# Projection products of a hybrid S5 and DeltaNet layer, split by rows into two halves of TensorE's array

## The chip, the cores and the metric

The kernel runs on one core of one Trainium2 chip. The metric is the device time of one execution in microseconds. Three executions of the kernel before took 3030.34, 3026.27 and 3029.54 us: a median of 3029.54 us. A core has five engines that work at the same time, each with its own queue of instructions that it takes in order: PE (TensorE, matrix products; its loads of the stationary operand have a row of their own in the profile, PEld), DVE (VectorE), ACT (ScalarE), POOL (GpSimd) and SP (SyncE, which here issues the transfers). PE writes its products to PSUM, eight banks of 128 partitions by 512 float32 values; DVE and ACT read them from there.

## The reference

The layer maps x, 1024 frames of 2048 channels in float32, to an output of the same shape:

```python
h = rmsnorm(x, ln_w)
proj = h @ w_in                      # 2048 -> 2048 + 4096 + 16 + 4096 columns
(u_s, z_s, q, k, v, z_d, beta_l, a_l, gate_s, gate_d) = split(proj)
y_s = s5_mixer(u_s, z_s, ...) @ s5_w_up        # diagonal state space, GELU, y * sigmoid(y @ w_glu), * silu(z)
y_d = deltanet_mixer(q, k, v, z_d, ...) @ dn_w_up   # causal conv, delta rule in chunks, 8 heads x 128
mixed = sigmoid(gate_s) * y_s + sigmoid(gate_d) * y_d
out = rmsnorm(x + mixed @ w_out, final_norm_w)
```

So there are the large matrix products (`w_in`, `w_glu`, `s5_w_up`, `dn_w_up`, `w_out`), and between them two mixers made of many small products, scans and elementwise work.

## The kernel before

**Tiles.** The 1024 frames are done in two passes of 512 (`NPASS`, `T`). In a pass the projections are 128 output channels at a time: the stationary operand is a 128x128 block of a weight (128 input rows, 128 output columns), the moving operand 128 rows of the activations by 512 frames, and one PSUM bank (`pb`) gathers the sum over 16 row blocks (8 for the second-level products `ud`, `us`, `glu`). To keep nearly float32 accuracy with the one-pass type float32r, the weight and the activation are each split into a high and a low part, `wh + wl` and `mh + ml`, and each block takes three products, `wh*mh`, `wh*ml`, `wl*mh` (lines 1515 to 1517), each with a weight load of its own. Below, a *large product* is one of these: 128x128 stationary, 512 columns moving. Without the first tile `k` and the narrow tile `ba`, the projections of both passes have 159 tiles of 48 and 80 tiles of 24 large products: 9,552. The last stage, `mixed @ w_out` (lines 1606 to 1649), has 1,536 more, with the activations stationary.

**Weights.** `w_load` (line 393) brings half a tile's weight block of 512 KB by a DMA on SP's queue, with three buffers. `w_prep` (line 404) makes the high part on ACT (`whi`) and the low part on DVE (`wlo`), in chunks of four row blocks, at most four chunks ahead of PE (`LA`).

**Epilogues.** When a tile's sum is complete, ACT and DVE take it from its bank. `conv_epi` (q, k, v): ACT copies it to `xpad` and, scaled, to `acc`, then DVE adds three shifted terms. `silu_epi` (z): ACT makes a tanh from the bank, DVE multiplies with the bank. `s5_epi` (u): ACT copies with a reordering. `gd`, `gs`, `glu`: a tanh on ACT. `ud`, `us`: one DVE instruction. Tiles take banks 0 and 1 in turn (`mainb`), so one bank is emptied while PE fills the other.

**Mixers between the products.** The small work stands in generators: `s5_gen` (banks 6 and 7), `d_prep` (banks 5 and 2) and `d_chain` (banks 3 and 4). After each row block of a projection `pump` lets each lane do a step when the planner's own clocks (`Clock`, `Timed`) say that its inputs are there; `drain` forces the rest at fixed places. The order in every engine's queue is fixed when the program is built. Thus short products of the mixers stand between the large ones on PE, in its one queue. `d_prep` transposes k (`pK`), sums squares of q with a one-column product (`pQ`), and forms k*k and k*q (`pA`) and a blockwise inverse with products of 32 and 64 rows (`pG`, `pU`); `d_chain` carries the state through four chunks (`pA`, `pB`, `pC`). The S5 branch has two groups for each half of a block: `pV`, products of 64 rows that alternate between rows 0-63 and 64-127 of the array and between banks 6 and 7, and `pY`, a full-row product and products with 64 output columns.

The parts of the planner's cost table and of the steps that matter here:

```python
elif k["rhs"].dtype == F32R:
    c = n / 2400                     # us that the planner books for a large product
...
pb = bank(mainb[0] % 2)              # a tile's sum
...
pA = bank((5, 2)[hf])                # d_prep; pK, pV, pU in bank 2, pD, pQ, pG in bank 5
return bank((3, 4)[bi[0] % 2])       # d_chain: every product in the other bank
```

Of the kernel before, what the change touches and what calls it, by code (L numbers as in the profile page):

```python
# [93 lines left out]
class Timed:  # L94
# [3 lines left out]
    def __getattr__(self, name):  # L98
        f = getattr(self.eng, name)
        if name not in COST:  # L100
            return f

        def g(*a, **k):
            o = a[0]
            ck = self.clock
            n = o.free_size()
            ins = [v for v in a[1:] if isinstance(v, bass.AP)]
            ins += [v for kk, v in k.items() if isinstance(v, bass.AP) and kk != "accum_out"]
            outs = [o]
            if self.key == "PE":  # L110
                if name == "transpose":
                    c = 0.11
                elif k["rhs"].dtype == F32R:
                    c = n / 2400
                else:
                    rows = k["lhsT"].shape[0]
                    c = max(n / 600, 0.06) * (0.3 if o.shape[0] <= 32 else 0.5 if min(o.shape[0], rows) <= 64 else 1.0)
                lat = 0.1
            elif name == "dma_start":
                c, lat = 4.0 * n * o.shape[0], 0  # L120
            else:
# [12 lines left out]
            ck.run(self.key, c, outs, ins, lat, name == "dma_start")  # L134
            return f(*a, **k)  # L135
        return g
# [11 lines left out]
def kernel(  # L148
# [724 lines left out]
    def s5_epi(pb, t):  # L873

        u = s5w["u"].rearrange("p (e n) -> p e n", e=2)
        S.activation(u, pb.rearrange("p (n e) -> p e n", e=2), AF.Copy)
        yield
        for q in range(4):
            SP.dma_start(part(us_d, t * 65536 + q % 2 * 32768 + q // 2 * 256, (512, 32), (16384, 2), (1, 256)),
                         u[32 * q:32 * q + 32])  # L880
        done.add(("u", t))
        yield -1
# [207 lines left out]
    def d_prep(h, ps_):  # L1090
# [16 lines left out]
        yield from until((ps_, "q", h))  # L1107
        pK = bank(2)
        S.activation(LU, kq[:, :, 1, :], AF.Square)
# [18 lines left out]
        for hf in range(2):  # L1128
            pA = bank((5, 2)[hf])
            for c in (2 * hf, 2 * hf + 1):  # L1130
                PE.matmul(pA[:, (c % 2) * 256:(c % 2) * 256 + 256], lhsT=kq[:, c, 0, :],
                          rhs=kq[:, c].rearrange("p a n -> p (a n)"), start=True, stop=True)
            pa = pA.rearrange("p (c a n) -> p c a n", c=2, a=2)
            tt(LU[:, 2 * hf:2 * hf + 2, :], pa[:, :, 0, :], E[:, 2 * hf:2 * hf + 2, :], MUL)
            tt(qk[:, 2 * hf:2 * hf + 2, :], pa[:, :, 1, :], E[:, 2 * hf:2 * hf + 2, :], MUL)
            yield
# [30 lines left out]
        yield from until((ps_, "v", h))  # L1167
        pV = bank(2)
        for c in range(4):
# [17 lines left out]
        yield  # L1187
        pU = bank(2)
        for b in B4:
# [18 lines left out]
        yield  # L1208
        pU = bank(2)
        pu = pU.rearrange("p (c n) -> p c n", c=4)  # L1210
# [18 lines left out]
        yield  # L1229
        pU = bank(2)  # L1230
        pu = pU.rearrange("p (c n) -> p c n", c=4)
# [8 lines left out]
    def d_chain(h, ps_):  # L1240
# [18 lines left out]
        zz = kq[:, 0:2].rearrange("p c a n -> p (c a n)")  # L1259
        bi = [0]  # L1260

        def bk():
            bi[0] += 1
            return bank((3, 4)[bi[0] % 2])
        for c in range(4):
# [109 lines left out]
    for ps_ in range(NPASS):  # L1375
# [39 lines left out]
        def silu_epi(pb, dst, split):  # L1415
            S.activation(th, pb, AF.Tanh, scale=0.5)
            yield
            if split:
                stt(eo(tx), by_step(th), 1.0, by_step(pb), ADD, MUL)
            else:  # L1420
                stt(tx, th, 1.0, pb, ADD, MUL)
            later(dst, tx)
            yield -1

        for kind, i, c0 in plan[ps_]:
# [22 lines left out]
            if not (ps_ == 0 and kind == "k" and i == 0):  # L1448
                pb = bank(mainb[0] % 2)
                mainb[0] += 1  # L1450
            if ps_ == 0 and kind == "ba":
                pk0 = bank(1)
                mainb[0] += 1

# [3 lines left out]
                for z in range(2):  # L1458
                    PE.matmul(pb[0:32, :], lhsT=ztile[:, 0:32], rhs=ztile, start=(z == 0), stop=False)
                    PE.matmul(pk0, lhsT=ztile[:, 0:P], rhs=ztile, start=(z == 0), stop=False)  # L1460
# [12 lines left out]
                for n, (kt, t0, nt) in enumerate(steps):  # L1473
# [17 lines left out]
                    wh, wl = hi[:, kl * P:(kl + 1) * P], lo[:, kl * P:(kl + 1) * P]  # L1491
                    PE.matmul(pb[0:32, cs], lhsT=h3[:, kl, 0:32], rhs=mh, start=False, stop=False)
                    PE.matmul(pb[0:32, cs], lhsT=h3[:, kl, 0:32], rhs=ml, start=False, stop=(n + 1 == len(steps)))
                    PE.matmul(pk0[:, cs], lhsT=wh, rhs=mh, start=False, stop=False)
# [3 lines left out]
            elif ps_ == 0 and kind == "k" and i == 0:  # L1498
                nkt, pb = 0, pk0
            for k4 in range(nkt // 4):  # L1500
                hi, lo = w_next()
                if kind == "ba":
                    h3 = hi.rearrange("p (k c) -> p k c", k=4)
                    for kl in range(4):
                        kt = k4 * 4 + kl
                        mh, ml = mov(kind, kt)
                        PE.matmul(pb[0:32, :], lhsT=h3[:, kl, 0:32], rhs=mh, start=(kt == 0), stop=False)
                        PE.matmul(pb[0:32, :], lhsT=h3[:, kl, 0:32], rhs=ml, start=False, stop=(kt == nkt - 1))
# [26 lines left out]
            if kind == "ba":  # L1535
                lgr = dw["set"][1]["kd"].rearrange("p c n -> p (c n)")[0:32, :] if ps_ == 0 else \
                    s5w["AB"][0:32, 0:512]
                S.activation(lgr, pb[0:32, :], AF.Copy)
                add("prep", -1, gates_prep(lgr, ps_))
# [28 lines left out]
            elif kind == "gd":  # L1568
                S.activation(q4[i % 2], pb, AF.Tanh, scale=0.5)
                later(td_d[i], q4[i % 2])  # L1570
            elif kind == "gs":
                S.activation(eo(q4[i % 2]), by_step(pb), AF.Tanh, scale=0.5)
                later(ts_d[i], q4[i % 2])
            elif kind == "ud":
                stt(mixed[:, i, :], q4[i % 4], 1.0, pb, ADD, MUL)
            elif kind == "glu":
                S.activation(q4[0], pb, AF.Tanh, scale=0.25)
                yh, yl = kt_of(yg, i)
# [5 lines left out]
            elif kind == "us":  # L1584
                stt(q4[3], q4[i % 3], 1.0, pb, ADD, MUL)
                tt(by_step(mixed[:, i, :]), by_step(mixed[:, i, :]), eo(q4[3]), ADD)
# [96 lines left out]
```

## Time and profile before

| What | Value |
|---|---|
| Median of three executions | 3029.54 us |
| Profiled execution, its own time | 3029.73 us |
| Its span, first to last instruction | 3027.8 us |
| Mean granted TensorE clock | 0.993 |
| PE busy | 2974.2 us, 98% |
| PEld busy | 2391.6 us, 79% |
| DVE busy | 1662.4 us, 55% |
| ACT busy | 1152.2 us, 38% |
| POOL busy | 449.3 us, 15% |
| PE's share of the chain that ended last | 85% |

The span is 1.9 us shorter than the execution's own time. A PE instruction's time in the profile runs from its start to its modelled end, and PE starts the next one before that end; what an instruction costs in a row of equal ones is thus the distance between two starts, which the timeline of the trace gives, not its mean duration. The timeline merges equal instructions that follow each other into one row with their count. The name of a row is what is written, an arrow, and what is read: `p<-X,whi` is a product into a PSUM bank from the activations in X and a high weight. `128*128 128x512` is rows by columns of the array that it uses, then the moving operand's rows by columns; all compute instructions carry the line of one recording helper, L135. A float32 product (not float32r) of the mixers stands in the trace as two PE instructions.

### The profile page before, as it was taken

What the parts mean: (1) busy time and instruction counts of PE and PEld (TensorE: products, weight loads), DVE (VectorE), ACT (ScalarE), POOL (GpSimd) and SP (SyncE); (2) the same over time, 40 slices, a digit from 0 to 9 for tenths busy, and PEclk for the clock granted to TensorE, in tenths of its full rate; (3) what the DMA queues carried; (4) which work ended last, traced back from release to release, by engine and by line L of the source; (5) the groups of instructions that cost most, each with busy time, mean ns of one, the idle gap of its engine ahead of it and who ended that gap; (6) DMA issues with size and microseconds to landing.
All of it is one profiled execution on the core that took longest, in us unless ns stands there. A gap on an engine that the chain in (4) does not pass through costs nothing.

```text
span 3027.8 us, 42544 instructions
## 1 busy us (share of the span) xinstructions
PE 2974.2 (98%) x16030; PEld 2391.6 (79%) x16030; DVE 1662.4 (55%) x3082; ACT 1152.2 (38%) x2483; POOL 449.3 (15%) x857
## 2 busy tenths in 40 slices
PE   8989999999999999999999999999999999999998
PEld 6877777777777888888878777777777788888887
DVE  5746676777777522553454575567557633226542
ACT  5434544554454222334333333333433322223331
POOL 4412222122200000000033221222112000000000
PEclk9999999999999999999999999999999999999999
DMA  6525444444445644446354344444444464445541
GB/s 168 133 57 154 122 121 130 111 117 122 133 135 166 191 122 120 144 134 238 119 160 134 108 114 115 133 114 117 119 126 120 123 207 122 122 122 153 197 151 56
DMA packets 582143, 405.02 MB, mean 134 GB/s; under 512 B 55161, under 2 KB 515122, under 8 KB 580018
## 3 DMA queue, kind: packets, MB, share of 16 engines
q1 hardware_dynamic: 579634, 393.92, 45.3%
q0 software_dynamic: 2304, 8.39, 0.8%
q8 instruction: 126, 2.06, 0.3%
q14 instruction: 79, 0.65, 0.1%
HBM read 335.66 MB, written 66.58 MB: 133 GB/s over the span
## 4 chain that ended last, share of the span: by engine, by line
PE 85%; DVE 7%; POOL 2%; ACT 2%; issue 1%; DMA 1%; SPq 0%; DVEq 0%; POOLq 0%; ACTq 0%
PE p L135 85%; DVE G0a L135 2%; POOL M L135 2%; DVE M L135 2%; DVE wlo L135 1%; DVE tmp L135 1%; ACT M L135 1%; DMA raw<-in_w_in_dram 0%; DVE Y L135 0%; POOL smalls L135 0%; DMA M<-tu_d 0%; SPq L135 0%; ACT whi L135 0%; ACT L135 0%; ACT tmp L135 0%
## 5 line engine op out<-in xcount | busy, mean ns | idle before, releaser
L135 PE MATMUL p<-X,whi 128*128 128x512 f32 (+1 forms) x4432 | 1398.7, 398 | 1.9 <-DVE whi L135 0.8
L135 DVE TENSOR_TENSOR wlo<-raw,whi 128x512 fp32r<-128x512 f32 x920 | 631.0, 698 | 700.9 <-ACT whi L135 700.1
L135 PEld LDWEIGHTS p<-X,whi 128*128 128x128 f32 (+1 forms) x4432 | 802.8, 188 | 177.1 <-issue 19.9
L135 PE MATMUL p<-X,wlo 128*128 128x512 f32 (+1 forms) x2184 | 854.2, 391 | 8.0 <-DVE wlo L135 7.9
L135 ACT ACTIVATE whi<-raw 128x512 fp32r<-128x512 f32 x917 | 557.7, 625 | 512.6 <-PE p L135 485.0
L135 PE MATMUL p<-Y,whi 128*128 128x512 f32 (+1 forms) x1808 | 568.8, 396 | 1.9 <-ACT whi L135 1.1
L135 PEld LDWEIGHTS p<-X,wlo 128*128 128x128 f32 x2184 | 411.7, 189 | 97.6 <-DVE wlo L135 9.1
L135 PEld LDWEIGHTS p<-Y,whi 128*128 128x128 f32 (+1 forms) x1808 | 329.9, 187 | 72.8 <-ACT whi L135 2.6
L135 PE MATMUL p<-Y,wlo 128*128 128x512 f32 x896 | 349.8, 390 | 0.0
L135 POOL TENSOR_SCALAR smalls<-smalls 128x4 f32<-128x4 f32 (+1 forms) x58 | 15.7, 270 | 1603.8 <-DVE smalls L135 1109.4
L135 ACT ACTIVATE tmp<-p 128x512 f32<-128x512 f32 x160 | 95.5, 597 | 401.8 <-PE p L135 391.9
L135 POOL TENSOR_TENSOR M<-M 32x28 f32<-32x28 f32 (+8 forms) x492 | 190.7, 388 | 289.4 <-DMA M<-lu_d 194.2
L135 DVE TENSOR_TENSOR G0a<-G0a 128x256 f32<-128x256 f32 (+1 forms) x432 | 212.3, 528 | 3.4
L135 PEld LDWEIGHTS p<-M 32*32 32x32 f32 (+2 forms) x3072 | 153.5, 123 | 72.6 <-ACT M L135 32.7
L135 PEld LDWEIGHTS p<-Y,wlo 128*128 128x128 f32 x896 | 168.3, 188 | 36.5 <-DVE wlo L135 0.4
L135 PE MATMUL p<-M 32*32 32x32 f32 (+3 forms) x3072 | 187.2, 215 | 7.5 <-ACT M L135 3.8
L135 ACT ACTIVATE M<-p 32x128 f32<-32x128 f32 (+3 forms) x337 | 99.3, 298 | 159.9 <-PE p L135 156.2
L135 DVE SCALAR_TENSOR_TENSOR tmp<-tmp,vec 128x512 f32<-128x512 f32 x144 | 115.6, 803 | 11.9 <-ACT tmp L135 8.5
L135 DVE TENSOR_TENSOR_SCAN G0a<-rho,scar,G0a 128x256 f32<-128x256 f32 x128 | 89.7, 742 | 0.0
L135 DVE TENSOR_TENSOR G0a<-p,G0a 128x512 f32<-128x512 f32 x128 | 82.0, 682 | 13.4 <-PE p L135 10.8
L135 PE MATMUL p<-whi,G0a 128*128 128x512 f32 x280 | 88.5, 391 | 0.0
L135 PE MATMUL p<-whi,X 128*128 128x512 f32 x256 | 82.2, 393 | 0.0
(210 smaller groups left out, 2655.4 us busy)
## 6 DMA issues: line engine op xcount, KB each, us to landing
raw<-in_w_in_dram SPq DMA_DIRECT2D x324, 512.0 KB, 4.0
raw<-in_w_out_dram SPq DMA_DIRECT2D x56, 512.0 KB, 3.9
raw<-in_dn_w_up_dram SPq DMA_DIRECT2D x32, 512.0 KB, 4.1
raw<-in_s_w_up_dram SPq DMA_DIRECT2D x32, 512.0 KB, 3.8
td_d<-tmp SPq DMA_DIRECT2D x32, 256.0 KB, 2.0
M<-tu_d SPq DMA_DIRECT2D x32, 256.0 KB, 3.8
cs_d<-G0a SPq DMA_DIRECT2D x32, 256.0 KB, 2.3
yg_d<-G0a SPq DMA_DIRECT2D x64, 128.0 KB, 2.4
```

The lines of the kernel that those rows point to most:

```text
L135: return f(*a, **k)
```

## The change

Each large product of the projections becomes two: input rows 0-63 and rows 64-127 of the same 128x128 weight block and of the same activations. The two use the upper and the lower half of the array's rows, and each half sums into a PSUM bank of its own, `pb[0]` and `pb[1]`. The work of a pair is that of one large product before; 9,552 large products become 19,104, and as many weight loads. The tile `ba`, the first tile `k` and the last stage `w_out` stay as they are.

The two halves are summed in the epilogue (`whole`): ACT copies the first bank, DVE adds the second. That is an added ACT copy and an added DVE addition for each of the 239 tiles, but for conv, whose two readings of the bank become a copy, an addition and a scaled copy from SBUF, and u, which had its copy already.

A tile takes two banks, 0 and 1 or 2 and 3 in turn. For that, `d_prep` has bank 5 alone, `d_chain` bank 4 alone, and the last stage's four sums take banks 0 to 3. The planner books half the time for a product of 64 rows.

```diff
-                    c = n / 2400
+                    c = n / 2400 * (0.5 if k["lhsT"].shape[0] <= 64 else 1.0)
...
-        S.activation(u, pb.rearrange("p (n e) -> p e n", e=2), AF.Copy)
+        pb = [z.rearrange("p (n e) -> p e n", e=2) for z in pb]
+        S.activation(u, pb[0], AF.Copy)
+        yield
+        tt(u, u, pb[1], ADD)
         yield
...
-        pK = bank(2)
+        pK = bank(5)
...
-            pA = bank((5, 2)[hf])
+            pA = bank(5)
...
-        pU = bank(2)
+        pU = bank(5)
...
         def bk():
-            bi[0] += 1
-            return bank((3, 4)[bi[0] % 2])
+            return bank(4)
...
+        def whole(o, pb):
+
+            S.activation(o, pb[0], AF.Copy)
+            if len(pb) == 2:
+                tt(o, pb[1], o, ADD)
+
         def conv_epi(pb, tile_i, dst, key):
-            S.activation(xpad[:, 3:515], pb, AF.Copy)
-            S.activation(acc, pb, AF.Copy, scale=vec[:, CONV + 72 + tile_i:CONV + 73 + tile_i])
+            whole(xpad[:, 3:515], pb)
+            S.activation(acc, xpad[:, 3:515], AF.Copy, scale=vec[:, CONV + 72 + tile_i:CONV + 73 + tile_i])
...
         def silu_epi(pb, dst, split):
-            S.activation(th, pb, AF.Tanh, scale=0.5)
+            whole(acc, pb)
+            yield
+            S.activation(th, acc, AF.Tanh, scale=0.5)
...
-                pb = bank(mainb[0] % 2)
+                pb = [bank(2 * (mainb[0] % 2) + c) for c in range(1 if kind == "ba" else 2)]
...
-                    PE.matmul(pb, lhsT=wh, rhs=mh, start=(kt == 0), stop=False)
-                    PE.matmul(pb, lhsT=wh, rhs=ml, start=False, stop=False)
-                    PE.matmul(pb, lhsT=wl, rhs=mh, start=False, stop=(kt == nkt - 1))
+
+                    for n, (w, m) in enumerate(((wh, mh), (wh, ml), (wl, mh))):
+                        for z in range(2):
+                            PE.matmul(pb[z], lhsT=w[64 * z:64 * z + 64, :], rhs=m[64 * z:64 * z + 64, :],
+                                      start=(kt == 0 and n == 0), stop=(kt == nkt - 1 and n == 2))
                     pump()
...
             elif kind == "ud":
-                stt(mixed[:, i, :], q4[i % 4], 1.0, pb, ADD, MUL)
+                whole(q4[(i + 3) % 4], pb)
+                stt(mixed[:, i, :], q4[i % 4], 1.0, q4[(i + 3) % 4], ADD, MUL)
             elif kind == "glu":
-                S.activation(q4[0], pb, AF.Tanh, scale=0.25)
+                whole(q4[0], pb)
+                S.activation(q4[0], q4[0], AF.Tanh, scale=0.25)
...
-            pbs = [bank((mainb[0] % 2, 3, 4, 1 - mainb[0] % 2)[t]) for t in range(4)]
+            pbs = [bank((2 * mainb[0] + t) % 4) for t in range(4)]
...
-                jb = bank((2, 5)[t % 2])
+                jb = bank(4 + t % 2)
```

The order of the built program shows it on PE, at two places of the first DeltaNet head in the first pass. In these rows `p0` to `p7` are the PSUM banks, `X0` and `X1` the activations, `whi` and `wlo` the weight's parts, `M0` the DeltaNet work area; `x2` is two equal instructions.

The first place is PE's queue ahead of the transposes of k (`ident`, four of them). Before:

```order
L135 MATMUL p0_113_969<-X1_7_172,wlo_112_933 128x512
L135 MATMUL p5_101_847<-dhl_169,after_r_101 128x256
L135 MATMUL p0_113_969<-X1_7_172,whi_114_970 128x512 x2
L135 MATMUL p0_113_969<-X1_7_172,wlo_115_971 128x512
L135 MATMUL p2_124_1053<-ident_75,M0_64_531 128x128 x4
```

With the change:

```order
L135 MATMUL p0_129_1304<-X1_7_172,wlo_128_1263 128x512
L135 MATMUL p1_130_1305<-X1_7_172,wlo_128_1263 128x512
L135 MATMUL p5_138_1403<-ident_75,M0_64_531 128x128 x4
L135 MATMUL p0_129_1304<-X1_7_172,whi_131_1306 128x512
L135 MATMUL p1_130_1305<-X1_7_172,whi_131_1306 128x512
```

Each large product became two neighbours that write banks 0 and 1; the transposes, which use all 128 rows, now stand between products of 64 rows, and they write bank 5 in place of bank 2.

The second place is PE's queue ahead of the one-column products (`ones`, `pQ` in the code), twelve large products behind those transposes, where one tile has just ended and the next begun. Before:

```order
L135 MATMUL p0_113_969<-X1_7_172,whi_114_970 128x512 x2
L135 MATMUL p0_113_969<-X1_7_172,wlo_115_971 128x512
L135 MATMUL p1_125_1077<-X0_6_171,whi_117_998 128x512 x2
L135 MATMUL p1_125_1077<-X0_6_171,wlo_118_999 128x512
L135 MATMUL p5_128_1085<-ones_80,M0_64_531 128x1 x4
```

With the change:

```order
L135 MATMUL p0_129_1304<-X1_7_172,wlo_132_1307 128x512
L135 MATMUL p1_130_1305<-X1_7_172,wlo_132_1307 128x512
L135 MATMUL p5_142_1447<-ones_80,M0_64_531 128x1 x4
L135 MATMUL p2_143_1459<-X0_6_171,whi_134_1336 128x512
L135 MATMUL p3_144_1460<-X0_6_171,whi_134_1336 128x512
```

The one-column products write bank 5 as before, but bank 5 is now also the bank that ACT and DVE read the transposes from; and the next tile goes to banks 2 and 3.

Over the whole program, the shape in which the array is used changes between neighbouring products on PE at 399 places before and at 1,051 with the change: 374 times from 64 rows to all 128 and 342 times back (32 times each before), the rest among the mixers' shapes. In this count float32r products of 32 columns and transposes stand for the full width, since no spacing in the trace of before sets them apart from it.

More of the change, by code (lines that the diff above doesn't have):

```diff
@@ L1167, in d_prep @@
         yield from until((ps_, "v", h))
-        pV = bank(2)
+        pV = bank(5)
         for c in range(4):
@@ L1208, in d_prep @@
         yield
-        pU = bank(2)
+        pU = bank(5)
         pu = pU.rearrange("p (c n) -> p c n", c=4)
@@ L1229, in d_prep @@
         yield
-        pU = bank(2)
+        pU = bank(5)
         pu = pU.rearrange("p (c n) -> p c n", c=4)
@@ L1259, in d_chain @@
         zz = kq[:, 0:2].rearrange("p c a n -> p (c a n)")
-        bi = [0]
         def bk():
-            bi[0] += 1
-            return bank((3, 4)[bi[0] % 2])
+            return bank(4)
         for c in range(4):
@@ L1415, in silu_epi @@
         def silu_epi(pb, dst, split):
-            S.activation(th, pb, AF.Tanh, scale=0.5)
+            whole(acc, pb)
+            yield
+            S.activation(th, acc, AF.Tanh, scale=0.5)
             yield
             if split:
-                stt(eo(tx), by_step(th), 1.0, by_step(pb), ADD, MUL)
+                stt(eo(tx), by_step(th), 1.0, by_step(acc), ADD, MUL)
             else:
-                stt(tx, th, 1.0, pb, ADD, MUL)
+                stt(tx, th, 1.0, acc, ADD, MUL)
             later(dst, tx)
@@ L1452 @@
                 pk0 = bank(1)
-                mainb[0] += 1
                 steps = [(kt, t0, 2) for t0 in (0, 2) for kt in range(8)]
@@ L1458 @@
                 for z in range(2):
-                    PE.matmul(pb[0:32, :], lhsT=ztile[:, 0:32], rhs=ztile, start=(z == 0), stop=False)
+                    PE.matmul(pb[0][0:32, :], lhsT=ztile[:, 0:32], rhs=ztile, start=(z == 0), stop=False)
                     PE.matmul(pk0, lhsT=ztile[:, 0:P], rhs=ztile, start=(z == 0), stop=False)
@@ L1491 @@
                     wh, wl = hi[:, kl * P:(kl + 1) * P], lo[:, kl * P:(kl + 1) * P]
-                    PE.matmul(pb[0:32, cs], lhsT=h3[:, kl, 0:32], rhs=mh, start=False, stop=False)
-                    PE.matmul(pb[0:32, cs], lhsT=h3[:, kl, 0:32], rhs=ml, start=False, stop=(n + 1 == len(steps)))
+                    PE.matmul(pb[0][0:32, cs], lhsT=h3[:, kl, 0:32], rhs=mh, start=False, stop=False)
+                    PE.matmul(pb[0][0:32, cs], lhsT=h3[:, kl, 0:32], rhs=ml, start=False, stop=(n + 1 == len(steps)))
                     PE.matmul(pk0[:, cs], lhsT=wh, rhs=mh, start=False, stop=False)
@@ L1498 @@
             elif ps_ == 0 and kind == "k" and i == 0:
-                nkt, pb = 0, pk0
+                nkt, pb = 0, [pk0]
             for k4 in range(nkt // 4):
@@ L1506 @@
                         mh, ml = mov(kind, kt)
-                        PE.matmul(pb[0:32, :], lhsT=h3[:, kl, 0:32], rhs=mh, start=(kt == 0), stop=False)
-                        PE.matmul(pb[0:32, :], lhsT=h3[:, kl, 0:32], rhs=ml, start=False, stop=(kt == nkt - 1))
+                        PE.matmul(pb[0][0:32, :], lhsT=h3[:, kl, 0:32], rhs=mh, start=(kt == 0), stop=False)
+                        PE.matmul(pb[0][0:32, :], lhsT=h3[:, kl, 0:32], rhs=ml, start=False, stop=(kt == nkt - 1))
                         pump()
@@ L1537 @@
                     s5w["AB"][0:32, 0:512]
-                S.activation(lgr, pb[0:32, :], AF.Copy)
+                S.activation(lgr, pb[0][0:32, :], AF.Copy)
                 add("prep", -1, gates_prep(lgr, ps_))
@@ L1568 @@
             elif kind == "gd":
-                S.activation(q4[i % 2], pb, AF.Tanh, scale=0.5)
+                whole(q4[i % 2], pb)
+                S.activation(q4[i % 2], q4[i % 2], AF.Tanh, scale=0.5)
                 later(td_d[i], q4[i % 2])
             elif kind == "gs":
-                S.activation(eo(q4[i % 2]), by_step(pb), AF.Tanh, scale=0.5)
-                later(ts_d[i], q4[i % 2])
+                whole(q4[i % 2], pb)
+                S.activation(eo(q4[2 + i % 2]), by_step(q4[i % 2]), AF.Tanh, scale=0.5)
+                later(ts_d[i], q4[2 + i % 2])
             elif kind == "ud":
-                stt(mixed[:, i, :], q4[i % 4], 1.0, pb, ADD, MUL)
+                whole(q4[(i + 3) % 4], pb)
+                stt(mixed[:, i, :], q4[i % 4], 1.0, q4[(i + 3) % 4], ADD, MUL)
             elif kind == "glu":
-                S.activation(q4[0], pb, AF.Tanh, scale=0.25)
+                whole(q4[0], pb)
+                S.activation(q4[0], q4[0], AF.Tanh, scale=0.25)
                 yh, yl = kt_of(yg, i)
@@ L1584 @@
             elif kind == "us":
-                stt(q4[3], q4[i % 3], 1.0, pb, ADD, MUL)
+                whole(q4[3], pb)
+                stt(q4[3], q4[i % 3], 1.0, q4[3], ADD, MUL)
                 tt(by_step(mixed[:, i, :]), by_step(mixed[:, i, :]), eo(q4[3]), ADD)
```

## The prediction, made before the change was run

> **What bounds the kernel now.** I read the page first: the engines' shares, the granted clock by slices, the chain that ended last.
>
> ```profile
> PE 2974.2 (98%) x16030; PEld 2391.6 (79%) x16030; DVE 1662.4 (55%) x3082; ACT 1152.2 (38%) x2483; POOL 449.3 (15%) x857
> PEclk9999999999999999999999999999999999999999
> ...
> PE 85%; DVE 7%; POOL 2%; ACT 2%; issue 1%; DMA 1%; SPq 0%; DVEq 0%; POOLq 0%; ACTq 0%
> ```
>
> PE is busy throughout, at full clock, and is 85% of the chain. So the time is PE's queue: the distances between the starts of its products, added up. Second view: PE's timeline in a stretch with large products alone.
>
> ```profile
> 1200.75 0.39 PE L135 MATMUL p<-X,wlo 128*128 128x512 f32 x1
> 1200.98 0.62 PE L135 MATMUL p<-X,whi 128*128 128x512 f32 x2
> 1201.43 0.39 PE L135 MATMUL p<-X,wlo 128*128 128x512 f32 x1
> 1201.66 0.62 PE L135 MATMUL p<-X,whi 128*128 128x512 f32 x2
> 1202.11 0.39 PE L135 MATMUL p<-X,wlo 128*128 128x512 f32 x1
> ```
>
> From 1200.75 to 1202.11 are 1.36 us and six products: 0.227 us each. That is what a large product costs, whatever its own row says (0.39). Third view: PE around a `pV` group of the S5 branch, the one place where the kernel already does what the change does: products of 64 rows that alternate between the halves of the array, each half with its own bank.
>
> ```profile
> 886.50 0.61 PE L135 MATMUL p<-X,whi 128*128 128x512 f32 x2
> 886.96 0.39 PE L135 MATMUL p<-X,wlo 128*128 128x512 f32 x1
> 887.27 1.14 PE L135 MATMUL p<-G0b 64*128 64x256 f32 x8
> 888.34 0.73 PE L135 MATMUL p<-X,whi 128*128 128x512 f32 x2
> 888.91 0.39 PE L135 MATMUL p<-X,wlo 128*128 128x512 f32 x1
> ```
>
> The weight loads of the same stretch:
>
> ```profile
> 886.73 0.19 PEld L135 LDWEIGHTS p<-X,wlo 128*128 128x128 f32 x1
> 887.27 0.73 PEld L135 LDWEIGHTS p<-G0b 64*128 64x128 f32 x8 [0.35 <-issue]
> 888.34 0.30 PEld L135 LDWEIGHTS p<-X,whi 128*128 128x128 f32 x2 [0.33 <-ACT G0a L135]
> ```
>
> And a `pY` group, with float32 instructions of the same 256 columns on the whole array (`x2`) and on halves of its columns (`x8`):
>
> ```profile
> 2118.13 0.39 PE L135 MATMUL p<-X,wlo 128*128 128x512 f32 x1
> 2118.36 0.59 PE L135 MATMUL p<-G0b,G0a 128*128 128x256 f32 x2
> 2118.88 1.09 PE L135 MATMUL p<-G0a,G0b 128*64 128x256 f32 x8
> 2119.90 0.73 PE L135 MATMUL p<-X,whi 128*128 128x512 f32 x2
> 2120.47 0.39 PE L135 MATMUL p<-X,wlo 128*128 128x512 f32 x1
> ```
>
> Three things are to be seen. First, halves overlap. The two whole-array instructions take 0.59; with a tail like a large product's 0.39 less 0.227, so about 0.16, they are some 0.215 apart. Eight in a row would need 1.72; the eight of 64 rows are over in 1.14, with a weight load and a tail in it. A pair thus takes one product's place, 0.216. Second, the load at 886.73 lies wholly under the products that run from 886.50 to 887.11: weight loads are hidden already. Third, there is a hole on each side of the group: no load for 0.35 us before it and 0.33 after it.
>
> **The change part by part.** *The pairs.* 9,552 large products at 0.227 become 9,552 pairs. The trace of before has no float32r product of 64 rows, so their price is bounded. From below: the float32 pair's 0.216, which would save 9,552 x 0.011 = 105 us. From above: no overlap, 0.454, which would add 2,168. I take 0.227. In float32 the split changed nothing (0.215 whole, 0.216 as a pair); the 0.011 by which a float32r product of 512 columns is dearer than a float32 one of 256 goes with the type or the stream, and each half still streams 512 columns of float32r. Issue is no bound: products of 32 rows, each with a load of its own, come much faster than two in 0.227.
>
> ```profile
> L135 PE MATMUL p<-M 32*32 32x32 f32 x2304 | 64.6, 193 | 2.4 <-DMA M<-tu_d 1.9 <-ACT M L135 0.2
> ```
>
> 64.6 us for 2,304 is 0.028 each. Term: 0, from -105 to +2,168.
>
> Two rules of the Trainium skill speak for the change. Its page "TensorE: Matmul & The Clock Gate" says, under "Back-to-back issue gap", that warm products start N/2.4 + 2.5 ns apart, and under "Part 3: Packing small matmuls — row/col tiling" that tiles on different rows overlap with about 4 ns for each further one. By these a pair would take 0.220, an estimate, and the saving would be 67 us; the trace agrees for float32, and not for the large products, which stand at 0.227 and not 0.216. The same part says that a weight load overlaps a product in flight only where the row groups differ; by that rule every load of before would lie bare and the split would hide it. The load at 886.73 lies under whole-array products, so the trace does not agree, and no term comes of it.
>
> *Changes of the array's shape.* From the low product at 886.96 to that at 888.91 are 1.95 us. Three large products (0.68) and four pairs (0.86) make 1.54; 0.41 is left for two changes of shape, 0.20 each. Around `pY`: 2.34 from 2118.13 to 2120.47, less 0.68 and six places of 0.215 (1.29), leaves 0.37, so 0.18 each. A group of `d_chain` that keeps the shape:
>
> ```profile
> 302.36 0.40 PE L135 MATMUL p<-X,wlo 128*128 128x512 f32 x1
> 302.59 0.38 PE L135 MATMUL p<-M 128*128 128x128 f32 x2
> 302.73 0.71 PE L135 MATMUL p<-X,whi 128*128 128x512 f32 x2
> 303.28 0.40 PE L135 MATMUL p<-X,wlo 128*128 128x512 f32 x1
> ```
>
> 0.92 from 302.36 to 303.28, less 0.68 and two half-width instructions (0.215), leaves 0.02. So a group that kept the shape before and now stands between products of 64 rows pays 0.41 in place of 0.02: 0.19 for each change. In the order of the built program changes go from 399 to 1,051: transposes, `pQ`, `pA`, `d_chain` and `pY`'s first product each stand in the pair stream now, while `pV` no longer differs from it. Term: 652 x 0.19 = +124 us, from 652 x 0.17 = 111 to 652 x 0.20 = 130.
>
> *One bank for each mixer stage.* `pQ` used another bank than the transposes ahead of it. PE around one:
>
> ```profile
> 1983.30 0.39 PE L135 MATMUL p<-X,wlo 128*128 128x512 f32 x1
> 1985.42 1.05 PE L135 MATMUL p<-ones,M 128*128 128x1 f32 x8 [1.73 <-ACT M L135]
> ```
>
> ACT at that place, the square of q and the last square of the transposed k:
>
> ```profile
> 1984.73 0.63 ACT L135 ACTIVATE M<-M 128x512 f32<-128x512 f32 x1 [3.29 <-DVE M L135]
> 1986.02 0.28 ACT L135 ACTIVATE M<-p 128x128 f32<-128x128 f32 x1
> ```
>
> and DVE, which reads the transposes last:
>
> ```profile
> 1986.43 0.69 DVE L135 TENSOR_TENSOR M<-p,ex 128x512 f32<-128x512 f32 x1 [1.73 <-ACT M L135]
> ```
>
> PE waited for ACT's squares of q (ended 1985.36). With bank 5 for both it also waits until the transposes have been read: DVE's product ends at 1987.12, 1.7 us later, with all large products queued behind. Sixteen heads: 0 to 27 us. `pA`'s second half now waits for two DVE readings of the first:
>
> ```profile
> L135 DVE TENSOR_TENSOR M<-p,M 128x256 f32<-128x256 f32 x64 | 24.1, 419 | 57.1 <-PE p L135 57.1
> ```
>
> 2 x 0.42 x 16 = 13 at most. Slower PE work ahead of these places gives ACT and DVE time, so I take +20, from 0 to 40. `d_chain`'s next product needs the previous one's result anyway: 0.
>
> *Epilogues.* A copy on ACT and an addition on DVE for most tiles:
>
> ```profile
> L135 ACT ACTIVATE tmp<-p 128x512 f32<-128x512 f32 x160 | 95.5, 597 | 401.8 <-PE p L135 391.9 <-DVE M L135 4.7 <-DVE G0a L135 2.3
> L135 DVE TENSOR_TENSOR G0a<-p,G0a 128x512 f32<-128x512 f32 x128 | 82.0, 682 | 13.4 <-PE p L135 10.8 <-DMA raw<-in_w_in_dram 2.6
> ```
>
> 1.3 us a tile, under the next tile's 24 or 48 products (5.4 or 10.9 us), which go to the other pair of banks. The tightest stretch for DVE is `ud` in the first pass:
>
> ```profile
> 850.00:935.00 85.00, 84.48 (x396) 67.18 (x395) 63.44 (x139) 42.12 (x75) 2.27 (x3) 1.00 0.54 155
> ```
>
> 63.4 of 85 us on DVE (the third engine's column), 16 tiles add 11: 88%, still below PE. Without that cover, if DVE became the bound, 239 x 0.68 = 163 us more DVE work would come onto the path. Only the last `glu` tile, whose result `us` needs at once, is not covered: at most 1.3 in each pass, +2.
>
> Sum: 3029.7 + 0 + 124 + 20 + 2 = **3176 us**, against the profiled execution's 3029.7, which stands at the median of the runs (3029.5).
>
> **The rivals.** *Pairs at 0.216* (25%). For it: the float32 pair, and that the extra 0.011 may be a gap between two products that the other half fills. Against it: both halves stream at once, so what slows one slows both. 3176 - 105 = 3071, slower still.
>
> *Pairs dearer than 0.227* (12%). The float32 pair passes 256 columns in 0.216, this one 512, on two halves into two banks. If reading or writing costs 6%, a pair takes 0.240: 9,552 x 0.013 = 124 more, 3300.
>
> *No overlap in float32r* (6%). 3176 + 2168 = 5344. No row speaks for it but that none shows such a pair.
>
> *Faster* (5%). Two halves that hide one another's gap, so 0.216, and changes of shape that cost only an emptying of the array, because the 64-row weights are loaded under the products ahead. The holes in the load row are 0.35 and 0.33, but the product of 0.73 for `x2` at 888.34, against 0.61 at 886.50, shows 0.12 of a change to be an uncovered load; without it a change costs some 0.08. Then 652 x 0.08 = 52, less 105: 2977, with the waits 2990. It decides once a change costs under 105/652 = 0.16. Against it: both prices of a change are above that, and the load after 64-row products waited too.
>
> *No difference* (2%): 0.216 with a change at 0.16.
>
> **How the numbers follow.** 50% for the sum, with its own range from 3145 to 3215 by its small terms. The range reaches down to take in the case of 3071 and up to that of 3300: 3055 to 3300, which leaves out the 5344, the faster and equal cases, and the edges of the two. Faster by over 0.2% (about what a measurement of this kernel can tell from no change) is 5%, within it 2%, slower 93%.
>
> **What would show it.** In the timeline of after, pairs in a quiet stretch: 0.227 from pair to pair by the sum, 0.216 or 0.24 by the rivals. Around a `d_chain` group, 0.4 us in place of 0.02, and load holes of 0.33 on both sides of each. `pQ` waiting longer, for DVE. PE nearly 100% busy, DVE near 57%, ACT near 40%. The prediction is wrong if pairs start more than 0.01 from 0.227, or if a change of shape between whole-array and 64-row products costs other than 0.17 to 0.20.

## The result, and the profile after

The changed kernel takes 3118.7 us (median of four runs, 3118.0 to 3122.6) against 3029.9 us before (3026.3 to 3031.5): 1.030 times the time, with an interval of 1.028 to 1.032. It is 89 us slower. The forecast was 3176 us, from 3055 to 3300. So the sign is as forecast and the loss is 57 us smaller than the sum said. The time lies below the sum's own range, 3145 to 3215, and inside the wide one.

The profiled execution takes 3118.7 us with a span of 3116.9. Its page gives busy time, share and instructions of each engine, and the chain of waits by engine:

```profile
PE 3077.0 (99%) x25582; PEld 2387.9 (77%) x25582; DVE 1800.5 (58%) x3321; ACT 1249.0 (40%) x2661; POOL 464.4 (15%) x857
...
PE 96%; DVE 1%; ACT 1%; POOL 1%; DMA 1%; issue 0%; DVEq 0%; POOLq 0%; SPq 0%; ACTq 0%
```

PE was 85% of the chain before and is 96% of it now; the time is still PE's queue. DVE at 58% and ACT at 40% are where the prediction saw them. The longer epilogues stand in two groups, DVE's addition and ACT's copy (busy us, mean ns of one, then the idle time ahead and what ended it):

```profile
L135 DVE TENSOR_TENSOR tmp<-p,tmp 128x512 f32<-128x512 f32 x223 | 153.4, 688 | 260.2 <-ACT tmp L135 256.6
L135 ACT ACTIVATE tmp<-p 128x512 f32<-128x512 f32 x224 | 133.9, 598 | 503.2 <-PE p L135 499.9
```

Now PE's timeline of the changed kernel, in the stretch that the prediction read (start, length, then the group; `x2` is one pair of halves):

```profile
1200.64 0.39 PE L135 MATMUL p<-X,wlo 64*128 64x512 f32 x2
1200.87 0.62 PE L135 MATMUL p<-X,whi 64*128 64x512 f32 x4
1201.32 0.39 PE L135 MATMUL p<-X,wlo 64*128 64x512 f32 x2
1201.55 0.62 PE L135 MATMUL p<-X,whi 64*128 64x512 f32 x4
1202.00 0.39 PE L135 MATMUL p<-X,wlo 64*128 64x512 f32 x2
```

From 1200.64 to 1202.00 are 1.36 us and six pairs, 0.227 each: exactly what six whole products took. The same view around a `d_chain` group of two products:

```profile
330.93 0.39 PE L135 MATMUL p<-X,wlo 64*128 64x512 f32 x2
331.25 0.49 PE L135 MATMUL p<-M 128*128 128x128 f32 x2
331.67 0.73 PE L135 MATMUL p<-X,whi 64*128 64x512 f32 x4
332.24 0.40 PE L135 MATMUL p<-X,wlo 64*128 64x512 f32 x2
```

1.31 us from low pair to low pair, where the group of the kernel before took 0.92. Less three pairs (0.68) and the group's own 0.215, 0.41 is left in place of 0.02: two changes of shape at 0.2. The weight loads at another such group show where it goes:

```profile
306.83 0.19 PEld L135 LDWEIGHTS p<-X,wlo 64*128 64x128 f32 x2
307.37 0.30 PEld L135 LDWEIGHTS p<-M 128*128 128x128 f32 x2 [0.35 <-ACT whi L135]
307.79 0.30 PEld L135 LDWEIGHTS p<-X,whi 64*128 64x128 f32 x4
```

Ahead of the group no load runs for 0.35 us; behind it there is a hole of 0.12 (307.67 to 307.79), and not the 0.33 that the prediction expected on that side as well. The `pV` group, which the change made the same shape as its neighbours, went the other way:

```profile
988.08 0.39 PE L135 MATMUL p<-X,wlo 64*128 64x512 f32 x2
988.31 1.02 PE L135 MATMUL p<-G0b 64*128 64x256 f32 x8
988.98 0.81 PE L135 MATMUL p<-X,whi 64*128 64x512 f32 x4
989.64 0.40 PE L135 MATMUL p<-X,wlo 64*128 64x512 f32 x2
```

1.56 us against 1.95 before: 0.39 saved by two changes fewer. The third thing that the prediction named, the wait of the one-column products (`ones`), did not come. Of before and of after, the idle time ahead of that tile's instructions on PE, loads included, by what ended it (us, times):

```profile
  ACT M L135: 22.2, 13
```

```profile
  issue: 3.2, 9
  DVE M L135: 0.7, 2
```

One wait can stand in such a count twice, on the row of loads and on that of products: of the 22.2 us for ACT before, 9.7 stand on the products' row, and that is PE's own idle time. After, 0.7 us for DVE are left, all on the row of loads.

To see all of it, every PE start of both traces was put into one of two sums: distances between neighbouring large products, and distances across a group of mixer products (from the last large product ahead of it to the first behind, with what that one's own distance has over 0.227; that 0.227 itself is in neither sum, nor is the start of the kernel). The first sum goes from 2305.8 to 2310.8 us, the second from 554.7 to 638.0: 83 of the 89 us lie around the mixers' groups. Of the 5 between large products, 4 are one wait for a weight's low part, 8.1 us long on the row of loads before and 12.3 after. Within the groups, the 20th percentile of each kind of group stands for a group without a wait: these sum to 518.2 before and 626.6 after, +108 us for 652 more changes. What lies above, the waits, falls from 36.5 to 11.5 us. So the profile says: changes of shape cost some 108 us, and waits that were there before gave 25 back. This split is an estimate, for a kind of group that occurs only a few times keeps its waits in the first part. The experiments test the parts.

### The profile page after: what moved, and what is told of

Read it like the earlier page. It is cut to its first block, busy times and chain, and to the rows that moved or that the text cites. A ratio compares the mean times of both kernels' runs of the same rounds, so it can differ in the third digit from the quotient of the medians.

```text
span 3116.9 us, 62098 instructions
## 1 busy us (share of the span) xinstructions
PE 3077.0 (99%) x25582; PEld 2387.9 (77%) x25582; DVE 1800.5 (58%) x3321; ACT 1249.0 (40%) x2661; POOL 464.4 (15%) x857
## 4 chain that ended last, share of the span: by engine, by line
PE 96%; DVE 1%; ACT 1%; POOL 1%; DMA 1%; issue 0%; DVEq 0%; POOLq 0%; SPq 0%; ACTq 0%
PE p L135 96%; ACT M L135 1%; POOL M L135 0%; DVE Y L135 0%; DMA raw<-in_w_in_dram 0%; DVE M L135 0%; DVE G0b L135 0%; ACT Y L135 0%; DMA M<-in_x_dram 0%; ACT G0b L135 0%; DVE wlo L135 0%; ACT L135 0%; POOL smalls L135 0%; DVE G0a L135 0%; ACT tmp L135 0%
## 5 line engine op out<-in xcount | busy, mean ns | idle before, releaser
L135 PE MATMUL p<-X,whi 64*128 64x512 f32 (+1 forms) x8752 | 1409.8, 398 | 1.9 <-DVE whi L135 0.8
L135 PEld LDWEIGHTS p<-X,whi 64*128 64x128 f32 (+1 forms) x8752 | 800.4, 184 | 203.8 <-issue 27.3
L135 PE MATMUL p<-X,wlo 64*128 64x512 f32 (+1 forms) x4344 | 854.4, 388 | 12.1 <-DVE wlo L135 12.1
L135 PE MATMUL p<-Y,whi 64*128 64x512 f32 (+1 forms) x3600 | 571.5, 394 | 0.7 <-ACT whi L135 0.7
L135 PEld LDWEIGHTS p<-X,wlo 64*128 64x128 f32 (+1 forms) x4344 | 411.0, 184 | 102.1 <-DVE wlo L135 13.5
L135 PEld LDWEIGHTS p<-Y,whi 64*128 64x128 f32 (+1 forms) x3600 | 330.9, 184 | 78.6 <-issue 5.6
L135 PE MATMUL p<-Y,wlo 64*128 64x512 f32 x1792 | 350.9, 387 | 0.1
L135 DVE TENSOR_TENSOR tmp<-p,tmp 128x512 f32<-128x512 f32 x223 | 153.4, 688 | 260.2 <-ACT tmp L135 256.6
L135 PEld LDWEIGHTS p<-Y,wlo 64*128 64x128 f32 x1792 | 168.8, 184 | 36.4 <-DVE wlo L135 0.9
L135 ACT ACTIVATE tmp<-tmp 128x512 f32<-128x512 f32 x160 | 102.1, 638 | 180.3 <-DVE tmp L135 179.9
```

## The experiments

Each ratio is against the kernel before, run on the same chip. The theory throughout: a pair costs what a whole product costs, the loss is the array's changes of shape, and the other parts of the change (banks, epilogues) are small.

**Whole products, all else of the change kept.** Same banks, same epilogues, and nearly the same order on PE; the first product of each triple goes to one bank, the other two to the second.

```diff
-                        for z in range(2):
-                            PE.matmul(pb[z], lhsT=w[64 * z:64 * z + 64, :], rhs=m[64 * z:64 * z + 64, :],
-                                      start=(kt == 0 and n == 0), stop=(kt == nkt - 1 and n == 2))
+                        PE.matmul(pb[min(n, 1)], lhsT=w, rhs=m, start=(kt == 0 and n < 2),
+                                  stop=(kt == nkt - 1 and n != 1))
```

> The changed kernel with whole-array products again, 128 rows each, in the same order on every engine: wh*mh goes to the tile's first bank, wh*ml and wl*mh to its second, and the epilogue with its copy and its addition, the single banks of the mixers and the planner's plan stay. The array's shape changes at 398 places in place of 1,051. Theory (the time came from the changes of shape, 108 us by the groups' distances in the trace, less waits of PE that they hid): 3118.7 - 108 = 3011, and between 0 and 45 us of waits at the mixers' products come back, so 3011 to 3056, with group waits above the 11 us of the changed kernel. Rival (the epilogues and the merged banks cost the time, the split little): above 3095.

Measured: 3033.8 us, ratio 1.0008 (0.9999 to 1.0017). The split alone thus costs 3118.7 - 3033.8 = 85 us, and banks and epilogues together 3.4 us beside the 3030.4 of the kernel before on that chip, at the edge of what can be told from nothing. The same two sums as above, between this kernel and the changed one: groups without a wait go from 507.6 to 626.6, +119 us for 653 changes (0.18 each), and waits from 44.2 to 11.5, -33. The difference, 86, is near the 85 that was timed. PE's order is not the same throughout: 329 of this kernel's 524 groups stand behind the same large product in both. In these alone the two parts are +78 us and -15 (waits 23.5 and 8.4), so the waits fall where the order is the same too. The one-column products show this cover in small. In this kernel they wait for DVE, as the prediction said they would (both rows counted; 2.3 us on that of the products):

```profile
  DVE M L135: 10.3, 16
```

In the changed kernel that wait is 0.7. The delays at the changes come ahead of it and give DVE the time.

**Pairs where no mixer is near.** As above, but the tiles of `gs`, `glu` and `us` are split by rows: 2,688 products become pairs, and there are only 3 changes of shape more.

```diff
+                        if kind not in ("gs", "glu", "us"):
+                            PE.matmul(pb[min(n, 1)], lhsT=w, rhs=m, start=(kt == 0 and n < 2),
+                                      stop=(kt == nkt - 1 and n != 1))
+                            continue
+                        for z in range(2):
+                            PE.matmul(pb[z], lhsT=w[64 * z:64 * z + 64, :], rhs=m[64 * z:64 * z + 64, :],
+                                      start=(kt == 0 and n == 0), stop=(kt == nkt - 1 and n == 2))
```

> As the kernel with whole-array products and two banks, but the tiles gs, glu and us, 2,688 of the 9,552 large products, split by rows into pairs, in a stretch where few mixer products stand; the array's shape changes at 401 places. Theory (a pair costs what a whole product costs, only changes of shape cost): within 5 us of the kernel with all products whole. Rival (each pair costs more, the 88.7 us of the change spread over 9,552 pairs, 0.0093 us each): 25 us slower than that kernel.

Measured: 3032.3 us, ratio 1.0005 (0.9995 to 1.0014), so -1.6 us beside the 3033.8 of whole products, within what can be told from nothing. Pairs by themselves cost and save nothing. In its timeline, six pairs again take 1.36 us:

```profile
1200.30 0.39 PE L135 MATMUL p<-X,wlo 64*128 64x512 f32 x2
...
1201.66 0.39 PE L135 MATMUL p<-X,wlo 64*128 64x512 f32 x2
```

**The price of a change, by itself.** Behind each of the 512 row blocks of the `gs` tiles stands one tiny product (128 rows, one column) whose result nobody reads. In the changed kernel this makes 1,018 changes of shape more; in the kernel of whole products, none.

```diff
+                    if kind == "gs":
+                        PE.matmul(bank(4)[:, 0:1], lhsT=ones, rhs=ones[:, 0:1], start=True, stop=True)
```

Among pairs:

> The changed kernel with a tiny whole-array product, 128 rows by one column, after each of the 512 row blocks of the tiles gs, into a bank that nothing reads: each stands between two pairs of 64 rows, so there are 1,018 more changes of the array's shape than in the changed kernel (2,069 against 1,051). Its own cost is measured apart, in the kernel with whole products and the same tiny products. Theory (a change costs 0.14 to 0.20 us, 0.14 by the one-column groups of the changed kernel and 0.20 by the float32 groups): 143 to 204 us above the changed kernel beside the tiny products' own cost. Rival (a change costs only the emptying of the array, 0.09 as between two starts): 92 us beside it.

Among whole products:

> The kernel with whole-array products and two banks, with the same 512 tiny products after the row blocks of the tiles gs: no more changes of shape than without them (398). It gives the tiny product's own cost: two float32 instructions whose weight loads of 128 columns set their pace, 0.11 us each by the one-column groups of before, so 512 x 0.22 = 113 us above the kernel without them, 3147.

Measured: 3386.5 us among pairs (ratio 1.1175, 1.1157 to 1.1194), 267.8 more than the changed kernel; 3151.8 us among whole products (1.0403, 1.0387 to 1.0418), 118.0 more than whole products alone. The difference, 149.8 us over 1,018 changes, is 0.147 us each. Both timelines show it in one row block, first among pairs, then among whole products:

```profile
1119.79 0.39 PE L135 MATMUL p<-X,wlo 64*128 64x512 f32 x2
1120.11 0.38 PE L135 MATMUL p<-ones 128*128 128x1 f32 x2
1120.42 0.73 PE L135 MATMUL p<-X,whi 64*128 64x512 f32 x4
1120.99 0.39 PE L135 MATMUL p<-X,wlo 64*128 64x512 f32 x2
```

```profile
1059.91 0.39 PE L135 MATMUL p<-X,wlo 128*128 128x512 f32 x1
1060.13 0.28 PE L135 MATMUL p<-ones 128*128 128x1 f32 x2
1060.27 0.71 PE L135 MATMUL p<-X,whi 128*128 128x512 f32 x2
1060.82 0.40 PE L135 MATMUL p<-X,wlo 128*128 128x512 f32 x1
```

1.20 us against 0.91: 0.29 for two changes. So a change costs by itself, with a product whose result nothing waits for; 149.8 lies in the theory's 143 to 204, and the rival of 92 falls. But beside a one-column product a change costs 0.147 and not the 0.19 of the prediction. The whole-product kernel suggests why: a one-column product does not last as long as the load behind it, so a part of that load lies bare there already, and a change pays for the rest only. That reading is argued from the rows, not shown.

**Single banks alone.** The kernel before, with the mixers' products in the single banks that the change gives them, and nothing else.

```diff
-        pK = bank(2)
+        pK = bank(5)
...
-            pA = bank((5, 2)[hf])
+            pA = bank(5)
...
-        pU = bank(2)
+        pU = bank(5)
...
-            return bank((3, 4)[bi[0] % 2])
+            return bank(4)
```

> The kernel before, with the mixers' products moved to the single banks that the change gives them (pK, pA, pV, pU to bank 5, the S5 and glu products of the other helper to bank 4), and nothing else: large products whole, one bank for each tile, old epilogues, margin 0.2. Theory (the term 'one bank for each mixer stage' was sized 0 to 40 us; whole products with single banks, two banks a tile and the new epilogues took 3033.8): the banks alone make 0 to 10 us at this margin, 3030 to 3040, and the one-column products wait on DVE in place of ACT. Rival (the prediction's size of the term): 20 us, about 3050.

(Bank 4 is that of `d_chain`, not of the S5 and glu products that the expectation names.)

Measured: 3057.2 us, ratio 1.0094 (1.0077 to 1.0110), 28 us slower than the kernel before. The theory of 0 to 10 us falls; the prediction's own size of the term, 20 us with bounds of 0 and 40, holds for the banks alone. Of its mechanism, one half is seen: the wait of the one-column products. On the row of products alone, before and with single banks:

```profile
  ACT M L135: 9.7, 6
```

```profile
  DVE M L135: 21.8, 7
```

That is 12 of the 28 us. `pA`, for which the prediction allowed up to 13, pays nothing: the middle one of its groups takes 1.10 us in both kernels. The rest lies where the prediction put 0, at `d_chain`. One place with single banks:

```profile
1856.41 0.35 DVE L135 SCALAR_TENSOR_TENSOR M<-p,negc,M 128x128 f32<-128x128 f32 x1 [0.69 <-PE p L135]
...
1856.67 0.40 PE L135 MATMUL p<-Y,wlo 128*128 128x512 f32 x1
1856.85 0.37 ACT L135 ACTIVATE M<-p,ex 128x128 f32<-128x128 f32 x1 [1.29 <-DVE M L135]
...
1857.27 0.49 PE L135 MATMUL p<-M 128*128 128x128 f32 x2 [0.21 <-ACT M L135]
```

DVE has the operand of the next product ready at 1856.76. But that product now writes the bank that ACT still reads until 1857.22, and it starts at 1857.27, 0.60 us behind the large product ahead of it; with two banks such a product started 0.23 behind (302.59 in the prediction's view). Over all groups of two such products, what they take above an undisturbed one is 18.0 us, where it was 2.6: 15 us more.

The kernel of whole products has this wait too, 16.7 us; there its 16 groups with one-column products take 14 us less than in the kernel before, which makes up for it. Why they do, the second bank of each large tile or the order that the planner sets with the longer epilogues, was not separated. The same groups of two show how the split covers a wait: the middle one takes 0.87 us with single banks, 0.87 with whole products and 0.87 with pairs, though an undisturbed one takes 0.45, 0.45 and 0.85. With pairs the changes of shape stand in place of the wait.

**The planner's margin.** If waits at these places are what the changes cover, then planning the mixers later should remove waits before the change and little after it. The margin that the planner adds behind a producer is 0.2 us; it was set to 1.0 and 0.5 in the kernel before:

```diff
-WAIT = 0.2
+WAIT = 1.0
```

> The kernel before with the planner's margin between a step and the next one of its lane at 1.0 us in place of 0.2; nothing else. PE's waits at groups of mixer products are 36 us in the kernel before and 11 in the changed one. Theory (these waits are there because steps are placed too early, and the changed kernel lost them because its changes of shape delayed PE): 3005 to 3020, group waits below 20 us. Rival (they come from ACT's and DVE's load and only move): 3025 to 3045, waits as before or found elsewhere.

Measured: 3017.1 us, ratio 0.9950 (0.9935 to 0.9965). The waits of weight loads on ACT's results in the DeltaNet area went from 45.6 to 3.8 us, but others came for the S5 branch (`G0b`):

```profile
PEld p L135 <- ACT G0b L135: 14.2, 11, 2.8
...
PEld p L135 <- ACT M L135: 3.8, 7, 0.8
```

Half of the expectation came true: the time is in its band and the waits it aimed at went, but a part of them turned up elsewhere, and by the two sums the waits at groups are 32 us and not below 20. With 0.5:

> The kernel before with the planner's margin at 0.5 us, between the 0.2 of before and the 1.0 that gave 3017. If the gain comes from giving ACT time before the DeltaNet products, half of it or all: 3010 to 3024, PE's waits for ACT at the DeltaNet work area between 46 us and 4. If 1.0 was a lucky order: 3025 or more.

Measured: 2997.6 us, ratio 0.9893 (0.9878 to 0.9908), 33 us faster than the kernel before, below both bands of the expectation, and the fastest version here that does all the work:

```profile
PEld p L135 <- ACT M L135: 12.7, 34, 0.8
...
PEld p L135 <- ACT G0b L135: 4.2, 5, 1.4
```

The loads' waits on ACT are 12.7 us in place of 45.6, and those for `G0b` stay small. These are idle times of the loads and not of PE: by the two sums, PE's waits at groups fall from 36.5 to 18.0 us. The planner also sets another order, with 501 groups in place of 523, so not all of the 33 us is shown to be waits. Then the same margin of 0.5 in the changed kernel, in the kernel of whole products, and in the kernel with single banks alone:

> The changed kernel with the planner's margin at 0.5 us; the array's shape changes at 1,006 places in it (1,051 with the margin of 0.2). Theory (the changed kernel's changes of shape had covered waits of PE, so the margin has little left to gain there: 45 changes fewer, some 8 us, and at most the 11 us of waits that are left): 3100 to 3113, and over the whole-array kernel with the same margin the bill of 607 changes in full, at 0.17 to 0.18 us each 100 to 110 us, against the 85 us between the two at a margin of 0.2. Rival (the margin gains the same 33 us as in the kernel before, so nothing was covered): 3086.

> The kernel with whole-array products and two banks for each tile, with the margin at 0.5 us; 399 changes of shape. Theory (single banks and added epilogue cost little once steps come late enough): 2997 to 3010, beside 2998 of the kernel before with that margin. Rival (the single banks make PE wait at the mixers whatever the margin): 3020 or more.

> The same with a margin of 0.5 in place of 0.2. The kernel before gains 32.7 us by that margin, whole products with the change's banks and epilogues only 8. Theory: the single banks hold the gain back, so this stands at 3020 to 3030, with the one-column products waiting on DVE for some 15 us. Rival: the second banks and longer epilogues of the large tiles hold it back, and this stands at 2995 to 3006 like the kernel before with that margin.

Measured: 3110.2 us with the whole change (ratio 1.0258, 1.0236 to 1.0280), 8.5 less than with 0.2. 3025.7 with whole products (0.9981, 0.9971 to 0.9991), 8.1 less. 3014.1 with single banks alone (0.9950, 0.9935 to 0.9964), 43 less than with 0.2, but 16.5 more than the kernel before with this margin. The first meets the theory's band: with the change in, there is little left to remove. The other half of that theory missed: over the kernel of whole products with the same margin the split costs 84.5 us, not the whole bill of 100 to 110. By the two sums it is +110 for the changes and -23 for waits, since 34 us of waits are still there with whole products at this margin. For whole products the theory missed and its rival was right: they stand 28 us above the 2997.6. For the third neither band was met; 3014 lies between them. If the parts add, single banks hold back 16.5 of these 28 us, and two banks a tile with their epilogues the other 11.6. The one-column products show the banks' part, both rows counted, first in the kernel of whole products, then with single banks alone (1.9 us in the kernel before with this margin):

```profile
  DVE M L135: 15.4, 14
```

```profile
  DVE M L135: 20.3, 17
```

**What the 0.227 of a product is made of.** The prediction left open whether the 0.011 us over a float32 instruction of half the width is a gap for each product or a slower stream. In the kernel before, the third product of each triple of the `w_out` stage took 320 of its 512 columns; the outputs of columns 320 to 511 lack that term, and the work of 512 products is shortened.

```diff
-                PE.matmul(pbs[t], lhsT=b, rhs=hi, start=False, stop=(kt == KT - 1))
+                PE.matmul(pbs[t][:, 0:320], lhsT=b, rhs=hi[:, 0:320], start=False, stop=(kt == KT - 1))
```

> The kernel before with the third of each three products in the last stage, the activations' low part by the weight's high part, done for 320 of 512 columns (columns 320 to 511 of each block lack this term; 512 - 64 = 448 to 512 products are shortened, those of all 8 column groups). It asks what the 0.0133 us is by which a float32r product of 512 columns takes longer (0.2267) than 512 columns at the rate of the float32 rows (0.2133). If it is a gap for each product: 0.1467 for 320 columns. If the stream itself is slower: 0.1417. The time falls by some 41 or 43 us.

Measured: 2997.2 us in a single run, 33.2 less and not 41 or 43, 0.065 for each of the 512. The timeline:

```profile
2879.97 0.39 PE L135 MATMUL p<-wlo,G0a 128*128 128x512 f32 x1
2880.20 0.54 PE L135 MATMUL p<-whi,G0a 128*128 128x320 f32 x2
...
2881.79 0.39 PE L135 MATMUL p<-wlo,G0a 128*128 128x512 f32 x1
2882.03 0.30 PE L135 MATMUL p<-whi,G0a 128*128 128x320 f32 x1
2882.17 0.40 PE L135 MATMUL p<-whi,G0b 128*128 128x512 f32 x1
```

Three triples in 1.82 us are 0.607 each; less two products of 0.227, a short one in a triple costs 0.153. A slower stream alone would give 0.227 x 320/512 = 0.142, a fixed gap of 0.011 some 0.147; both lie below. The single distances do not decide it either: in the trace's nanoseconds the short product itself takes 0.143 to the next start, as by the slower stream, and it is the two whole products of the triple that take longer, 0.231 and 0.233 in place of 0.227. Why they do stays open.

## Why the prediction was right, and where its sum was off

The sign, the size of a pair and the kind of the cost came out as reasoned. The range is another matter: half the chance went to the sum's own range of 3145 to 3215 (its terms' bounds add up to 3143 to 3202), and 3118.7 is below either. It lies in the wide range because that was drawn down to 3055 for the rival of pairs at 0.216, which is not what happened; to that extent it is luck that the range held. By the prediction's own sign it is also wrong in one point: next to one-column products a change of shape costs 0.14 to 0.15 us, outside 0.17 to 0.20.

*The pairs.* Right: 0.227 in the timeline of after, 0 us where they stand alone. With it fall the rivals at 0.216 (3071), at 0.24 (3300) and without overlap (5344), and the faster one, which needed 0.216 as well (its 2990 should read 2999, with the 22 us of the other terms). The reason given also stands: the loads were hidden before, and two halves with 512 columns each take the time of one product. The bound of 0.216 came from float32 products of 256 columns, half the width, and no row shows it for float32r products of 512.

*The changes of shape.* The step was right in kind and 5 to 16 us high: 652 x 0.19 = 124 against 119 beside the kernel of whole products, or 108 beside the kernel before. The error is that one price, read around float32 products of 128 and 256 columns, was given to all. In the undisturbed groups, two changes add 0.39 us to two products of `d_chain`, 0.40 to `pA` and 0.38 to a product of `dhl`, but 0.34 to four transposes and 0.28 to eight one-column products. Here is one of the last kind, 1.87 us from low pair to low pair:

```profile
2380.55 0.39 PE L135 MATMUL p<-Y,wlo 64*128 64x512 f32 x2
2380.87 1.05 PE L135 MATMUL p<-ones,M 128*128 128x1 f32 x8
2381.85 0.73 PE L135 MATMUL p<-Y,whi 64*128 64x512 f32 x4
2382.42 0.39 PE L135 MATMUL p<-Y,wlo 64*128 64x512 f32 x2
```

*One bank for each mixer stage.* This is the step that failed. Its size by itself was near, 28 us against 20, but only 12 of these come by the wait that was named; some 15 come from `d_chain`, put at 0 because its next product needs the previous one's result anyway. It needs DVE's reading of the bank; with one bank it also waits for ACT's, which ends later. The larger error is the term's place in the sum. With the rest of the change it costs, together with the epilogues, 3.4 us in place of 22. And once the split adds its delays, PE waits for the mixers' results 33 us less than with whole products. The prediction saw that slower PE work gives ACT and DVE time, and used it only to take the middle of the term's bounds; it never let the changes cover waits that were already there, 36.5 us around these groups in the kernel before. By these estimates the account closes: 5 us of the changes, 19 of banks and epilogues and 33 of cover make the 57 by which the forecast was high.

*The epilogues.* Taken at 2 us and covered, with DVE at 58% and ACT at 40%. They have no measurement of their own at the old margin, only within the 3.4. One wait that the change made longer is the one of 8.1 us for a weight's low part: it is 11.9 already with whole products, and whether the epilogues or the order cause that was not separated.

## What to carry to other kernels

Splitting a product that already fills all rows of the array gains nothing where its weight loads lie hidden: read the distance between starts, of whole products and of any pair of halves in the same trace, before splitting. Then count how often neighbours on PE will differ in shape, since each such place cost 0.14 to 0.2 us here, and small products scattered in a stream of large ones pay it twice each. Delays and waits at one place are not added: a delay ahead of a wait comes off it, so a term for a new wait is only worth what the other terms leave of it.

## What had not been expected

The planner's margin has its best value in the middle: 3029.9 us at 0.2, 2997.6 at 0.5, 3017.1 at 1.0, so a third of the change's loss could be had as a gain by one constant.

Two loads of 64 rows take no longer than one of 128: the row of `x2` at 306.83 above lasts 0.19 us, as the whole load at 886.73 in the kernel before. The halves' loads overlap just as their products do.

A float32r product of 320 columns in a triple makes the triple 0.01 us longer than its columns' share, and the extra stands in the distances of the whole products beside it, for a reason that no run here shows.
